# Hybrid mLSTM and stick-breaking layer: the fourth unit's low parts on VectorE in place of GpSimd, and the gates' small product at unit 6 in place of unit 4

## The chip, the cores and the metric

The kernel runs on one core of a Trainium2 chip. The metric is the device time of one execution in microseconds (us), given as the median of the runs. Besides the timed runs there is one profiled execution, from which the trace comes; times inside it count from the start of its span.

A core has TensorE (matmuls; PE in the profile, PEld for the loading of its stationary operand), VectorE (DVE), ScalarE (ACT), GpSimd (POOL) and SyncE (SP), which in this kernel issues nearly all DMAs. Each works through its own instructions in the order of the program, and semaphores make one wait for another.

## What is computed

One layer on x of 512 tokens by 1024 channels, in float32. The reference, cut to its main steps:

```python
h = rmsnorm(x, norm_w)
proj = einsum('bsd,de->bse', h, w_in) + b_in
(mq, mk, mv, mi, mf, mo, mz, sq, sk, sv, sz, gates) = split(proj, split_at)
qk = silu(causal_depthwise_conv(concat([mq, mk]), conv_w, conv_b))
hm = mlstm_chunkwise(q, k, mv, log_i=mi, log_f=log_sigmoid(mf))
y_m = rmsnorm_per_head(hm) * sigmoid(mo) * silu(mz)
os_ = stick_breaking_attention(rmsnorm(sq), rmsnorm(sk), sv)
y_s = os_ * silu(sz)
g_m, g_s = split(sigmoid(gates), 2)
merged = g_m * (y_m @ w_proj_m) + g_s * (y_s @ w_proj_s)
return x + merged @ w_out
```

`mi` and `mf` are four columns each of the input projection; the kernel calls their product the gates (`gates`), which are not the merge gates of the last lines.

## The kernel before

**Three matmuls for one.** Every product of float32 values is made from a high part (the value rounded by a ScalarE copy) and a low part (the value less its high part): high by high, high by low, low by high, added up in PSUM. So each weight tile is loaded by SyncE (`stg`), copied by ScalarE (`wh`) and subtracted by VectorE (`wl`, line 98); normalised x is kept as `hh` and `hl`.

**Units.** The weights are cut into units of 1024 x 128 or 256 x 512 elements, 24 matmuls of 512 columns each. The main loop runs over the units by number (c). In each round it first runs the work that is due at c (`later`, filled by `defer(n, fn)` for n rounds ahead, by `at`, or before the loop), splits the unit two ahead and loads the one four ahead (`ahead`), then issues the unit's matmuls in two halves, with a step of the attention heads between them. Functions due in one round run in the order in which they were put there. This order is the order on every engine.

**The first group.** Units 0 to 3 are the q columns of the attention's first set. They run differently: each token block (tb) takes all of k before the next, so that TensorE can start when the first block of x is normalised. Their weights are split by `first_split` (line 1140): two halves of a unit's tile, each a ScalarE copy (`fh`, line 1146) and a subtraction (`fl`, line 1147) by VectorE or by the engine given as `low`. Units 1 and 3 give GpSimd. Unit i holds k = 2i and 2i + 1, and every token block needs all eight. Around them VectorE and TensorE bring in x: `x_scale` (line 290 is the scaling; its root comes from GpSimd, lines 274 and 275), `x_turn` (line 300 the transposes on TensorE, 302 `hh`, 306 `hl`). The fourth unit's tile lies in the buffer `P5`. Line 347 adds the bias row (`brow`, DMA of line 311) to a finished token block.

**The gates.** `gates_prep` (lines 562 and 563, due at 3) lays the high and low parts of the eight columns into `wg`; `gates` (lines 573 to 581, due at `GATES_START`) multiplies them with `hh` and `hl` in 16 matmuls, copies one half by ScalarE (576), adds on VectorE (578) and stores the results by two SyncE DMAs (580, 581). `gates_scan` reads them from unit 35 on.

**What stands beside them.** The last q block is finished at unit 4. From there `SbSet.turn` runs: at unit 5 it transposes the first half of q on VectorE (`ty`, line 388), at unit 6 `move` sends it to `tz` by 16 SyncE DMAs (line 398), at unit 8 `weight` multiplies it on VectorE (line 402). The second half follows two units later: line 388 at 7, 398 at 8, 402 at 10. The bias row of k is also due at 6, and was put there before the gates. k's blocks are finished at unit 8 and scaled on VectorE (line 369, four steps a block): two blocks at 9, two at 10 behind that `weight`. In unit 10 the first head transposes k on TensorE (line 438).

Of the kernel before, what the change touches and what calls it, by code (L numbers as in the profile page):

```python
# [25 lines left out]

SB_START = [10, 13, 16, 20, 26, 28, 32, 34]
M_START = [52, 56, 70, 76]
GATES_PREP, GATES_START, GATES_SCAN = 3, 4, 35
TURNED = {("q", 0, 0), ("q", 0, 1), ("q", 1, 0), ("q", 1, 1), ("k", 0, 1), ("k", 1, 1)}  # L30
REST = {11, 16, 20, 23, 24, 32, 44, 64}
AHEAD, LOADS = 2, 4
# [3 lines left out]
def tile_hybrid_layer(  # L36
# [16 lines left out]
    nc = tc.nc  # L53
# [21 lines left out]
    def blk(tag, dt=F32, shape=(512,), name=None, p=128):  # L75

        where = mp if tag in MISC else sp
        return where.tile([p] + list(shape), dt, name=name or tag, tag=tag, bufs=BUFS[tag])

    def two(tag, dt=F32, name=None):  # L80

        t = blk(tag, dt, (2, 512), name=name)
        return t[:, 0, :], t[:, 1, :]
# [1057 lines left out]
    def first_split(i, low=None):  # L1141
        u = units[i]
        his = two("qk", FR, name="fh")
        for j in range(2):
            hi, lo = his[j], blk("y", FR, name="fl")
            nc.scalar.activation(hi, u.st[:, j, :], AF.Copy)
            (low or nc.vector).tensor_tensor(lo, u.st[:, j, :], hi.bitcast(F32), op=OP.subtract)  # L1147
            f_w.append((hi, lo))
# [25 lines left out]
    first_split(1, nc.gpsimd)  # L1174
    x_scale(1)
    first_split(2)
    first_split(3, nc.gpsimd)

    f_ps = []

# [121 lines left out]
```

## Time and profile before

| | us |
|---|---|
| median of 3 runs | 691.59 (691.51 to 693.78) |
| the profiled execution | 692.46 |
| its span | 690.7 |
| TensorE busy | 682.2 (99%) |
| VectorE busy | 467.5 (68%) |
| ScalarE busy | 337.1 (49%) |
| GpSimd busy | 115.3 (17%) |

The profiled execution's time is a little longer than its span, which runs from the first to the last instruction. TensorE is busy in nine tenths or more of all but the first and the last of the page's 40 slices. The chain of work that ended last is 94% TensorE's; its other parts lie in the first 38 us and at the end. A timeline row gives the start, the length, the engine, the line and the operation, output and inputs by name and shape; several equal instructions in a row stand as one with their count (x16), and their length is then that from the first start to the last end. In brackets stands how long the engine was idle before it, and who ended that.

### The profile page before, as it was taken

How to read it: one execution, taken by the hardware profiler on the slowest of the kernel's cores; microseconds unless marked ns; L12 is line 12 of the kernel's file. 1: busy time of each engine (PE TensorE's matmuls, PEld its weight loads, DVE VectorE, ACT ScalarE, POOL GpSimd, SP SyncE). 2: the span in 40 equal slices, each digit the busy share in tenths (PEclk: the TensorE clock that was granted, in tenths of full speed). 3: DMA queues.
4: the chain of work that ended last, by engine and by line, in shares of the span. 5: the costliest groups of instructions: out<-in, count | busy, mean ns of one | idle time of the engine just before them, and what ended most of it. 6: DMA issues, size and time to landing. Idle time of an engine off the chain costs nothing.

```text
span 690.7 us, 9388 instructions
## 1 busy us (share of the span) xinstructions
PE 682.2 (99%) x3162; PEld 568.9 (82%) x3162; DVE 467.5 (68%) x817; ACT 337.1 (49%) x631; POOL 115.3 (17%) x268
## 2 busy tenths in 40 slices
PE   7999999999999999999999999999999999999997
PEld 4878888888888888888888888888888888888876
DVE  6745687777997886679834748994352364445997
ACT  6235364576554663244466434447554343344451
POOL 5222022365440310000011110000112000111020
PEclk9999999999999999999999999999999999999999
DMA  7423534535553533553332333434323455489333
GB/s 249 138 92 107 155 108 127 148 71 151 158 149 106 135 106 90 112 121 92 106 108 61 91 105 104 117 92 125 88 62 91 113 179 196 135 194 222 121 82 102
DMA packets 122289, 84.74 MB, mean 123 GB/s; under 512 B 19018, under 2 KB 105956, under 8 KB 122240
## 3 DMA queue, kind: packets, MB, share of 16 engines
q1 hardware_dynamic: 119600, 77.97, 40.2%
q0 software_dynamic: 2496, 6.03, 4.5%
q8 instruction: 25, 0.41, 0.2%
q14 instruction: 24, 0.20, 0.1%
q10 hardware_dynamic: 144, 0.13, 0.1%
HBM read 66.22 MB, written 2.15 MB: 99 GB/s over the span
## 4 chain that ended last, share of the span: by engine, by line
PE 94%; DMA 2%; DVE 2%; POOL 1%; SPq 0%; ACT 0%; issue 0%; DVEq 0%; ACTq 0%
PE dps L92 27%; PE dps L93 27%; PE dps L94 27%; PE aps L93 3%; PE aps L94 3%; PE aps L92 3%; DMA P<-in_w_in_dram 1%; DMA brow<-in_b_in_dram 1%; PE aps L794 1%; PE aps L796 1%; PE aps L795 1%; DVE hl L306 1%; POOL fl L1147 0%; DVE hh L302 0%; DVE wl L98 0%; PE aps L573 0%
## 5 line engine op out<-in xcount | busy, mean ns | idle before, releaser
L98 DVE TENSOR_TENSOR wl<-stg,wh 128x1024 fp32r<-128x1024 f32 x92 | 112.6, 1224 | 107.6 <-ACT wh L97 107.4
L92 PE MATMUL dps<-hh,wh 128*128 128x512 f32 x448 | 175.0, 391 | 0.0
L94 PE MATMUL dps<-hh,wl 128*128 128x512 f32 x448 | 174.4, 389 | 0.0
L93 PE MATMUL dps<-hl,wh 128*128 128x512 f32 x448 | 174.4, 389 | 0.0
L97 ACT ACTIVATE wh<-stg 128x1024 fp32r<-128x1024 f32 x92 | 96.8, 1052 | 65.3 <-PE dps L94 45.1
L94 PEld LDWEIGHTS dps<-hh,wl 128*128 128x128 f32 x448 | 84.1, 188 | 17.7
L93 PEld LDWEIGHTS dps<-hl,wh 128*128 128x128 f32 x448 | 84.2, 188 | 16.8
L92 PEld LDWEIGHTS dps<-hh,wh 128*128 128x128 f32 x448 | 84.1, 188 | 16.8
L92 PE MATMUL dps<-wh,hh 128*128 128x512 f32 x224 | 87.7, 392 | 0.0
L94 PE MATMUL dps<-wh,hl 128*128 128x512 f32 x224 | 87.3, 390 | 0.0
L93 PE MATMUL dps<-wl,hh 128*128 128x512 f32 x224 | 87.2, 389 | 0.0
L94 PEld LDWEIGHTS dps<-wh,hl 128*128 128x128 f32 x224 | 42.0, 188 | 9.0
L92 PEld LDWEIGHTS dps<-wh,hh 128*128 128x128 f32 x224 | 42.1, 188 | 8.3
L93 PEld LDWEIGHTS dps<-wl,hh 128*128 128x128 f32 x224 | 42.1, 188 | 8.2
L687 DVE SCALAR_TENSOR_TENSOR acc<-tmp,vec,acc 128x511 f32<-128x511 f32 (+2 forms) x48 | 36.0, 750 | 1.7
L690 ACT ACTIVATE tmp<-acc 128x512 f32<-128x512 f32 x16 | 10.1, 634 | 50.8 <-DVE acc L687 50.8
L463 POOL TENSOR_SCALAR_AFFINE_SELECT om<-om 128x128 f32<-128x128 f32 x32 | 15.3, 479 | 96.2 <-ACT om L461 96.1
L469 DVE TENSOR_TENSOR_SCAN om<-om 128x512 f32<-128x512 f32 (+3 forms) x32 | 26.7, 834 | 5.5 <-POOL om L463 5.5
L747 POOL TENSOR_SCALAR_AFFINE_SELECT w_all<-om 128x128 f32<-128x128 f32 x16 | 5.7, 386 | 143.6 <-DMA om<-rb_d 129.4
L461 ACT ACTIVATE om<-aps,rq 128x512 f32<-128x512 f32 (+3 forms) x32 | 16.8, 524 | 21.0 <-PE aps L94 21.0
L92 PE MATMUL dps<-yh,wh 128*128 128x512 f32 x64 | 24.9, 389 | 0.0
L93 PE MATMUL dps<-yl,wh 128*128 128x512 f32 x64 | 24.9, 389 | 0.0
(249 smaller groups left out, 1222.2 us busy)
## 6 DMA issues: line engine op xcount, KB each, us to landing
stg<-in_w_in_dram SPq DMA_DIRECT2D x87, 512.0 KB, 3.9
az<-ay SPq DMA_DIRECT2D x128, 40.0 KB, 3.2
stg<-in_w_proj_s_dram SPq DMA_DIRECT2D x8, 512.0 KB, 4.3
B<-in_w_out_dram SPq DMA_DIRECT2D x8, 512.0 KB, 5.8
stg<-in_w_proj_m_dram SPq DMA_DIRECT2D x8, 512.0 KB, 5.5
wl<-stg POOLq DMA_DIRECT2D x8, 512.0 KB, 5.8
tz<-ty SPq DMA_DIRECT2D x72, 32.0 KB, 1.9
brow<-in_b_in_dram SPq DMA_DIRECT2D x8, 256.0 KB, 4.4
```

The costliest lines, as they stand in the source:

```text
L92: nc.tensor.matmul(ps, ah, bh, start=first, stop=False)
L93: nc.tensor.matmul(ps, ah, bl, start=False, stop=False)
L94: nc.tensor.matmul(ps, al, bh, start=False, stop=last)
L97: nc.scalar.activation(hi, src, AF.Copy)
L98: nc.vector.tensor_tensor(lo, src, hi.bitcast(F32), op=OP.subtract)
L306: nc.vector.scalar_tensor_tensor(hl[:, k, ts], tp[:, j * 128:(j + 1) * 128], nw_t[:, k:k + 1], hh[:, k, ts].bitcast(F32), op0=OP.mult, op1 ...
L461: nc.scalar.activation(om[:, 0:n], zp, AF.Sigmoid, scale=rn[:, h:h + 1])
L463: nc.gpsimd.affine_select(out=om[:, ts], in_=om[:, ts], compare_op=OP.is_gt, fill=1.0, base=0, channel_multiplier=1, pattern=[[-1, 128]])
L469: nc.vector.tensor_tensor_scan(back, back, back, 1.0, op0=OP.mult, op1=OP.bypass)
L687: nc.vector.scalar_tensor_tensor(acc[:, j:], t[:, 0:T - j], cw(3 - j, ch), acc[:, j:], op0=OP.mult, op1=OP.add)
L690: nc.scalar.activation(t, acc, AF.Sigmoid)
L794: nc.tensor.matmul(nm[:, 0:258], ph, vh, start=j == 0, stop=False)
```

## The change

Two edits. The fourth unit's low parts are made by VectorE, as the first and the third unit's are, and no longer by GpSimd. The gates' product, with all that `gates` issues, is due at unit 6 and no longer at unit 4; there it comes behind the bias row of k and ahead of `move`. Nothing else differs; what is computed is the same.

```diff
-GATES_PREP, GATES_START, GATES_SCAN = 3, 4, 35
+GATES_PREP, GATES_START, GATES_SCAN = 3, 6, 35
...
     first_split(1, nc.gpsimd)
     x_scale(1)
     first_split(2)
-    first_split(3, nc.gpsimd)
+    first_split(3)
```

## Rows read from the trace of the kernel before

**Rows 1.** Waits of TensorE, whole span: us in total, times, longest

```profile
PE aps L300 <- DVE x L290: 1.4, 2, 1.2
...
PE dps L1190 <- DVE fl L1147: 0.7, 1, 0.7
PE aps L573 <- DVE wg L563: 0.4, 1, 0.4
```

**Rows 2.** Timeline of TensorE, second half of the first unit: start, us

```profile
14.61 0.40 PE L1189 MATMUL dps<-fh,hl 128*128 128x512 f32 x1
...
16.83 0.50 PE L1190 MATMUL dps<-fl,hh 128*128 128x512 f32 x1 [0.73 <-DVE fl L1147]
...
18.55 0.39 PE L1188 MATMUL dps<-fh,hh 128*128 128x512 f32 x1
```

**Rows 3.** Timeline of VectorE and GpSimd, 6 to 18 us

```profile
6.83 1.29 DVE L1147 TENSOR_TENSOR fl<-stg,fh 128x512 fp32r<-128x512 f32 x2
...
12.90 3.32 POOL L1147 TENSOR_TENSOR fl<-P,fh 128x512 fp32r<-128x512 f32 x2 [0.30 <-ACT fh L1146]
13.31 3.46 DVE L1147 TENSOR_TENSOR fl<-stg,fh 128x512 fp32r<-128x512 f32 x2
16.31 0.51 POOL L274 TENSOR_SCALAR xs<-xs 128x1 f32<-128x1 f32 x1
16.70 0.68 DVE L302 TENSOR_TENSOR hh<-aps,nw_t 128x512 fp32r<-128x512 f32 x1
...
17.54 0.19 POOL L274 TENSOR_SCALAR xs<-xs 128x1 f32<-128x1 f32 x1
```

**Rows 4.** Timeline of TensorE around the gates' product

```profile
36.97 0.39 PE L1190 MATMUL dps<-fl,hh 128*128 128x512 f32 x1
37.77 0.47 PE L573 MATMUL aps<-hh,wg 128*128 128x512 f32 x1 [0.41 <-DVE wg L563]
...
41.50 0.39 PE L92 MATMUL dps<-wh,hh 128*128 128x512 f32 x1
```

**Rows 5.** Timeline of SyncE's DMA queue from the gates' stores on

```profile
43.10 0.28 SPq L580 DMA_DIRECT2D i_d<-g  x1
...
45.86 11.03 SPq L398 DMA_DIRECT2D tz<-ty  x16
56.99 1.04 SPq L117 DMA_DIRECT2D stg<-in_w_in_dram  x2
...
68.83 1.15 SPq L117 DMA_DIRECT2D stg<-in_w_in_dram  x2
```

**Rows 6.** Timeline of VectorE: weighting of q's second half, scaling of k

```profile
71.13 0.75 DVE L402 TENSOR_SCALAR tz<-tz,qkw 128x1024 f32<-128x1024 f32 x1
71.80 1.65 DVE L369 TENSOR_SCALAR kraw<-kraw,rk 128x128 f32<-128x128 f32 x8
```

**Rows 7.** Timeline of TensorE in unit 10

```profile
74.14 0.39 PE L92 MATMUL dps<-wh,hh 128*128 128x512 f32 x1
...
76.86 0.60 PE L438 MATMUL aps<-ident,kraw 128*128 128x128 f32 x4
77.22 0.48 PE L92 MATMUL dps<-wh,hh 128*128 128x512 f32 x1
```

**Rows 8.** Timeline of VectorE and TensorE, 20 to 23 us

```profile
20.21 1.41 DVE L290 TENSOR_SCALAR x<-x,xs 128x1024 f32<-128x1024 f32 x2
...
21.05 0.49 PEld L300 LDWEIGHTS aps<-ident,x 128*128 128x128 f32 x3
...
22.55 0.69 DVE L347 TENSOR_TENSOR qraw<-dps,brow 128x512 f32<-128x512 f32 x1 [0.94 <-DMA brow<-in_b_in_dram]
```

**Rows 9.** Timeline of VectorE: the low part of unit 5

```profile
34.80 1.23 DVE L98 TENSOR_TENSOR wl<-stg,wh 128x1024 fp32r<-128x1024 f32 x1 [2.79 <-ACT wh L97]
```

**Rows 10.** Moves (us to landing; ns), then the loads of 56.99 (us to landing)

```profile
DMA to landing us min/median/max: 1.9/1.9/1.9
L398 SPq DMA_DIRECT2D tz<-ty x48: 585/595/1287, 45.9 to 89.9; - x48
DMA to landing us min/median/max: 4.8/4.8/4.8
```

**Rows 11.** Timeline of TensorE at the start of the span

```profile
1.50 4.21 PE L1166 MATMUL dps<-idle 128*128 128x512 f32 x9 [1.50 <-DVE idle L1161]
```

## Prediction before the run

> **What bounds the kernel now.** I read the waits of TensorE first, since the page has it busy for 682.2 of 690.7 us: a change can pay only where TensorE stands still, and can cost only by making it stand still. The view has five entries in the whole span, all before 38 us, three of them shown; the change speaks to the last two [rows 1]. Next I read the timeline of those two places. In the second half of the first unit the matmuls that need the low parts `fl` come late: 14.61 and 18.55 are the starts of the 2nd and the 13th matmul from there [rows 2]. The reason stands beside it: VectorE's two subtractions take 3.46 us while GpSimd does two of its own in 3.32, and 1.29 when nothing runs beside them [rows 3]. The second place is the gates' product, whose first matmul waited 0.41 us for `wg` [rows 4]. Last I read SyncE's queue behind the gates' two stores, because the change puts those stores ahead of other DMAs [rows 5], and then who uses what these DMAs bring [rows 6, 7].
>
> **Low parts by VectorE: what it gives.** The two subtractions of the fourth unit (k 6 and 7) leave GpSimd and join VectorE's two (k 4 and 5). Four at 1.29 / 2 = 0.65 us are 2.6 us, so 13.31 + 2.6 = 15.9 in place of 16.70, where the next `hh` starts: VectorE is 0.8 us earlier although it does twice as much [rows 3]. For TensorE eleven matmul pitches lie between 14.61 and 18.55. Twelve matmuls from 74.14 to 76.86 give a pitch of 0.227 [rows 7], eleven are 2.50, and 3.94 were taken: 1.44 us to gain. The low parts are then ready at 14.0, 14.6, 15.3 and 15.9, the last needed at 16.9, so none is late. What is late next is the transpose of the third token block. TensorE came to it at 21.05 and would now come at 19.6; its input, the scaled `x`, is made from 20.21 on, now 0.8 earlier, and the first of the two takes half of 1.41: done at about 20.1 [rows 8]. So TensorE gains 21.05 - 20.15 = **0.9 us**, and I keep -0.1 to 1.44 as ends (the upper: `x` in time). VectorE itself keeps nothing: its addition at 22.55 waits for the bias row's DMA [rows 8], which SyncE issues as before, so everything from there on VectorE stands where it stood, and is still early enough for a TensorE that is 0.9 us ahead.
>
> [...] The row: one of GpSimd's one-column steps, 0.19 us at 17.54, took 0.51 at 16.31, where VectorE's subtractions had just ended [rows 3]. [...] The row has GpSimd as the one that is held. For the lower end I let two such steps of 0.51 each stop VectorE: 0.9 - 1.0 = -0.1.
>
> **The gates' product two units later: what it gives.** `gates` issues 16 matmuls, one ScalarE copy, one VectorE addition and two SyncE stores. At unit 4 its first matmul started at 37.77 where TensorE could have gone on at 36.97 + 0.23 = 37.20, and the block lasted 3.73 against 16 x 0.227 = 3.63 [rows 4]: 0.57 + 0.10 = **0.67 us** to gain. At unit 6 `wg` has long been there, and units 4 and 5 lie ready (unit 5's low part was made by 36.0 [rows 9], TensorE takes them at 36.3 and 41.7). Unit 4 starts at 37.20 - 0.9 = 36.3, the gates at 36.3 + 2 x 5.44 (24 matmuls each) = 47.2, unit 6 at 50.8 against 41.50 + 10.88 = 52.4. TensorE is 0.9 + 0.67 = **1.57 us ahead**. On ScalarE and VectorE the parts of unit 8 stand behind the gates' two steps, ready at about 54 and wanted at 61.7: hidden. This is the end of what the change gains.
>
> **What it moves on SyncE's queue: the price.** At unit 6 SyncE's order becomes the k bias row, the gates' two stores, and only then the 16 DMAs that move the turned q (first half), the loads of units 10 and 11, 16 more DMAs (second half), the loads of units 12 and 13. The first store, at 43.10, came 1.60 us after the gates' block ended; the two, at 0.28 each and the gaps behind them, hold the queue for some 0.7 [rows 4, 5]. After the change: 50.8 + 1.6 + 0.7 = 53.1 for the first move, where it was 45.86 [rows 5]. From 45.86 to 68.83 the queue issued one instruction after the other (16 moves in 11.03, two loads in 1.04, 16 moves), some 0.67 a move: a queue that is issue-bound doesn't catch up. Its last move was issued at 68.83 - 0.67 = 68.16, which is 22.3 after the first; now 53.1 + 22.3 = 75.4. It lands 1.9 later [rows 10], at 77.3. A move by itself takes 0.595 [rows 10]; if the gap behind it were half as long, 0.64 a move, it is 76.2; I take 77.1.
>
> On VectorE the weighting of that half (`weight`, line 402) stands ahead of the scaling of k's last two token blocks (line 369) in unit 10, and waits for all 16. It was at 71.13, with 1.1 us to spare after the landing at 70.0 [rows 6]; now it is at 77.1. The scaling starts 0.67 later and lasts 1.65; the transposes of k for the first head need the fifth of its eight steps, or the eighth if the wait is for all. TensorE's matmuls go on 1.85 to 2.45 after 77.1, say at 79.1. They went on at 77.22 [rows 7] and could at 77.22 - 1.57 = 75.65. **TensorE stands 3.5 us**, and the sum is 79.1 - 77.22 = **+1.9 us**. The ends: quick pace and fifth step, 78.05, +0.8; 77.3 and eighth step, 79.75, +2.5; with the other ends of the first gain +0.3 and +3.5.
>
> Cover that is used up on the way: the load of unit 10 goes out at 63.9 instead of 56.99, lands 4.8 later [rows 10], and its high and low parts (1.23 for the low [rows 9], the high taken as long) are done by 71.2; TensorE wants them at 74.14 - 1.57 = 72.6. Hidden by 1.4 us; were it gone, that stall would come before the one above and shorten it, not add to it. Unit 12's load, out at 76.1, is ready by the same count at 83.4, wanted at 77.22 + 36 x 0.227 + 1.9 = 87.3. Behind that the waits of the kernel before show no entry for TensorE to the end [rows 1], and I count nothing more.
>
> **Sum.** The profiled execution took 692.46 us (span 690.7), 0.87 above the median of 691.59. 692.46 - 1.57 + 3.5 = 694.4 in that execution's terms, **693.5** as a median. 0.5% is 3.46 us, about what a measurement of this kernel can tell from no change; 1.9 us is 0.27%.
>
> **Rivals.** *The queue doesn't hold TensorE*: the moves land by 73.5, issued quicker in a queue that holds no other transfer. Then only the gains are left, 692.46 - 1.57 = 690.9, 690.0 as a median. Against it: 32 moves beside 4.8-us loads and alone kept the same pace, and VectorE took these steps in the order of the program [rows 5, 6]. 14%.
>
> *The stall costs TensorE its clock*, the one that ends on the slower side. It decides from the point where TensorE stands still long enough in unit 10. The clock column of the page is 1.00 throughout, and the longest wait of TensorE in the part shown is 1.2 us [rows 1], so no row shows a stand of 3.5. [...] One such stretch here would lose half of it, 4.2 / 2 = 2.1 us: 1.9 + 2.1 = +4.0, 696.5, or 695.6 as a median. [...] 15%.
>
> *The first part gives nothing*: the four subtractions don't run at 0.65 (GpSimd's small steps, or the high parts, hold them) and TensorE is no earlier for it. Everything behind shifts with it: 1.9 + 0.9 = +2.8, 694.4 as a median. 9%.
>
> **How the numbers follow.** My forecast, a stall of 2.5 to 4.5 us in unit 10 that eats both gains, has 62%. The range reaches from the first rival's 690.0, less 0.2, to the second's 695.6 and 0.4 more: 689.8 to 696.0. Faster by over 0.5% (below 688.1) has no mechanism: 3% for what I overlooked. Slower by over 0.5% (above 695.05): most of the second rival, and a little from the upper ends of the others, 18%. The rest, 79%, lies within.
>
> **What would show it.** Right, step by step: VectorE's four low parts at 0.65 us from 13.3 on and no wait for `fl` among TensorE's; no wait for `wg`; the gates' stores at about 52.4 and the first move behind them at 53; `weight` at 77 with VectorE idle ahead of it for DMA; a new entry in TensorE's waits at about 75.5, 3 to 4 us for `kraw` of line 369; the clock column 1.00 there. Wrong: no such entry (the queue was quicker), a second entry for `wl` in units 10 to 13 (the loads came late as well), or matmuls at 0.43 behind the stall.

## The result, and the profile after

The changed kernel takes 1.0043 times as long as before (95% interval 1.0031 to 1.0054), about 3.0 us more; the medians are 695.3 and 691.61 us. One of the eight executions took 3680 us: it counts in the median of 695.3 and not in the ratio, and the other seven have a median of 694.93. The forecast was 693.5, +1.9 us: slower by less than 0.5%, and so it is, but by 1.1 us more than the sum said. The profiled execution took 695.68 us, its span is 694.0.

The waits of TensorE after, whole span (us in total, times, longest), to be held against rows 1:

```profile
PE aps L438 <- DVE kraw L369: 2.5, 2, 2.2
PE dps L1188 <- ACT fh L1146: 2.0, 1, 2.0
PE dps L1166 <- DVE idle L1161: 1.5, 1, 1.5
```

The waits for `fl` and for `wg` are gone. A new one has come first in the list: the transposes of k in unit 10 wait for its scaling. The second entry isn't the change's: in this execution the first weights landed later (the first high part at 7.31 us, 6.13 in the profile of before), ahead of anything that was edited. It isn't harmless, though. TensorE stood for it until 10.01, and with that the granted clock fell to 0.50, from about 10.0 to 13.4 by windows of half a us. First TensorE's row, then the windows (stretch, its length, busy time and count of PE, PEld, DVE, ACT and POOL, granted clock, DMA share, GB/s):

```profile
10.01 0.77 PE L1188 MATMUL dps<-fh,hh 128*128 128x512 f32 x1 [1.96 <-ACT fh L1146]
...
10.00:12.00 2.00, 1.99 (x5) 1.68 (x6) 1.96 (x7) 1.90 (x4) 1.95 (x2) 0.50 1.06 424
12.00:14.00 2.00, 2.00 (x8) 1.59 (x7) 1.88 (x6) 1.66 (x4) 0.75 (x2) 0.66 0.98 297
```

The gates' product began 1.2 us later in this execution than in a second one of the same kernel (47.53 and 46.35 us), whose clock did not fall there.

VectorE after, where rows 3 have GpSimd beside it:

```profile
13.57 1.29 DVE L1147 TENSOR_TENSOR fl<-stg,fh 128x512 fp32r<-128x512 f32 x2
14.78 1.29 DVE L1147 TENSOR_TENSOR fl<-P,fh 128x512 fp32r<-128x512 f32 x2
15.98 0.68 DVE L302 TENSOR_TENSOR hh<-aps,nw_t 128x512 fp32r<-128x512 f32 x1
```

Four subtractions in 2.5 us, where two took 3.46. Then SyncE's queue after, for rows 5:

```profile
52.76 0.28 SPq L580 DMA_DIRECT2D i_d<-g  x1
53.09 0.28 SPq L581 DMA_DIRECT2D f_d<-g  x1
53.41 10.35 SPq L398 DMA_DIRECT2D tz<-ty  x16
63.86 1.05 SPq L117 DMA_DIRECT2D stg<-in_w_in_dram  x2
65.01 10.65 SPq L398 DMA_DIRECT2D tz<-ty  x16
75.77 1.15 SPq L117 DMA_DIRECT2D stg<-in_w_in_dram  x2
```

The first move has gone from 45.86 to 53.41 and the order behind it is unchanged, so the last move is out at 75.7, where it was out at 68.7. VectorE, for rows 6, waits for the last of them, and the scaling of k waits with it:

```profile
77.22 0.75 DVE L402 TENSOR_SCALAR tz<-tz,qkw 128x1024 f32<-128x1024 f32 x1 [2.76 <-DMA tz<-ty]
77.89 1.65 DVE L369 TENSOR_SCALAR kraw<-kraw,rk 128x128 f32<-128x128 f32 x8
```

And TensorE in unit 10, for rows 7, where TensorE now stands waiting (the stand, for short):

```profile
75.64 0.38 PE L438 MATMUL aps<-ident,kraw 128*128 128x128 f32 x2
78.23 0.47 PE L438 MATMUL aps<-ident,kraw 128*128 128x128 f32 x1 [2.21 <-DVE kraw L369]
79.02 0.48 PE L438 MATMUL aps<-ident,kraw 128*128 128x128 f32 x1 [0.31 <-DVE kraw L369]
79.14 0.78 PE L92 MATMUL dps<-wh,hh 128*128 128x512 f32 x1
79.72 0.63 PE L93 MATMUL dps<-wl,hh 128*128 128x512 f32 x1
80.14 0.63 PE L94 MATMUL dps<-wh,hl 128*128 128x512 f32 x1
...
88.58 0.39 PE L92 MATMUL dps<-hh,wh 128*128 128x512 f32 x1
```

The transposes of the first two blocks run at once, the third waits for the first step of the scaling, the fourth for the fifth. The unit goes on at 79.14. But then the matmuls start 0.43 apart, not 0.227. The windows of this kernel show what goes with it (columns as above):

```profile
74.00:76.00 2.00, 2.00 (x10) 1.42 (x9) 0.46 (x1) 0.00 (x0) 0.00 (x0) 1.00 0.19 50
76.00:78.00 2.00, 0.02 (x1) 0.00 (x0) 0.78 (x2) 0.00 (x0) 0.00 (x0) 1.00 0.48 89
78.00:80.00 2.00, 1.46 (x4) 1.07 (x5) 1.54 (x8) 0.17 (x1) 0.00 (x0) 0.56 1.13 342
80.00:82.00 2.00, 2.00 (x7) 1.53 (x7) 1.09 (x1) 1.98 (x3) 0.00 (x0) 0.59 1.07 313
82.00:84.00 2.00, 2.00 (x10) 1.68 (x9) 2.00 (x6) 0.69 (x2) 0.00 (x0) 1.00 0.89 239
```

The granted clock fell again after the stand, to 0.50 from about 78.2 to 81.6 by windows of half a us. The 36 matmuls from the end of the stand to the next group's first (79.14 to 88.58) take 9.44 us. In the kernel before the same piece runs from 77.22 [rows 7] to 85.51, 8.29:

```profile
85.51 0.39 PE L92 MATMUL dps<-hh,wh 128*128 128x512 f32 x1
```

The lower clock cost 1.15 us here.

### The profile page after: what moved, and what is told of

It reads as the page before. It is cut to its first block, busy times and chain, and to the rows that moved or that the text cites. A ratio compares the mean times of both kernels' runs of the same rounds, so it can differ in the third digit from the quotient of the medians.

```text
span 694.0 us, 9385 instructions
## 1 busy us (share of the span) xinstructions
PE 684.4 (99%) x3162; PEld 571.3 (82%) x3162; DVE 466.3 (67%) x819; ACT 336.8 (49%) x631; POOL 111.8 (16%) x266
## 4 chain that ended last, share of the span: by engine, by line
PE 94%; SPq 3%; DMA 1%; issue 0%; DVE 0%; ACT 0%; DVEq 0%
PE dps L92 26%; PE dps L93 26%; PE dps L94 26%; PE aps L93 3%; PE aps L94 3%; PE aps L92 3%; SPq L398 3%; PE dps L1188 1%; PE dps L1189 1%; PE dps L1190 1%; DMA stg<-in_w_in_dram 1%; PE aps L794 1%; PE aps L796 1%; PE aps L795 1%; PE aps L300 0%
## 5 line engine op out<-in xcount | busy, mean ns | idle before, releaser
L94 PE MATMUL dps<-yh,wl 128*128 128x512 f32 x64 | 25.0, 391 | 0.0
```

Of the source, the lines that this page charges most:

```text
L94: nc.tensor.matmul(ps, al, bh, start=False, stop=last)
```

## Experiments

Two theories stood against each other at first. The queue: moving the gates' stores ahead of `move` holds 32 DMAs on SyncE, and the last of them holds TensorE. Its rivals: the work that the edits put on VectorE, or the edits simply adding up. Then a second question: whether the clock fell because of the stand. Ratios are to the kernel before, run on the same chip.

### One edit at a time

Only the low parts on VectorE:

```diff
-    first_split(3, nc.gpsimd)
+    first_split(3)
```

> Only the fourth unit's low parts go to VectorE; the gates' product stays at unit 4. Theory: TensorE comes about 0.9 us earlier to the end of the first group, but the gates' first matmul waits there for wg, whose time is set on VectorE by the bias row's DMA and stays at 37.7; so the gain goes into that wait (0.41 grows to about 1.2 us) and the time is that of the kernel before, within 0.3 us. Rival, that the two edits add up: 0.9 us faster, wait for wg unchanged. In either case the four low parts take 0.65 us each.

Measured: 1.0001 (0.9993 to 1.0010), 691.86 us. The four low parts take 0.65 us each and the wait for `fl` is gone, yet no time is gained. Two lines of TensorE's waits in this kernel:

```profile
PE aps L300 <- DVE x L290: 2.0, 2, 1.2
...
PE aps L573 <- DVE wg L563: 0.5, 1, 0.5
```

The wait for `wg` is there still, though not at the 1.2 us expected: in this execution the bias row landed 0.8 us earlier than in the profile of before (21.73 against 22.55 for the addition behind it), and `wg` with it. The direction holds: the edits do not simply add up. Only the gates' product at unit 6:

```diff
-GATES_PREP, GATES_START, GATES_SCAN = 3, 4, 35
+GATES_PREP, GATES_START, GATES_SCAN = 3, 6, 35
```

> Only the gates' product goes to unit 6; GpSimd keeps its low parts. Theory of the queue: TensorE gains 0.6 us at the place of the gates, the stores reach SyncE at about 53.3, the last of the 32 moves lands at about 78, and TensorE stands some 3.5 us in unit 10 for the scaling of k; 2.8 us slower than before, and 4 to 4.5 if the clock falls after the stand. Rival, that the stand in unit 10 comes from the first group's other split: no wait for kraw, 0.6 us faster.

Measured: 1.0055 (1.0043 to 1.0067), 3.8 us slower. SyncE's queue in this kernel:

```profile
52.98 0.28 SPq L580 DMA_DIRECT2D i_d<-g  x1
53.31 0.29 SPq L581 DMA_DIRECT2D f_d<-g  x1
53.63 10.32 SPq L398 DMA_DIRECT2D tz<-ty  x16
```

The moves start as late as in the changed kernel. Its transposes of k, on TensorE's timeline:

```profile
75.86 0.38 PE L438 MATMUL aps<-ident,kraw 128*128 128x128 f32 x2
78.36 0.33 PE L438 MATMUL aps<-ident,kraw 128*128 128x128 f32 x1 [2.12 <-DVE kraw L369]
79.15 0.33 PE L438 MATMUL aps<-ident,kraw 128*128 128x128 f32 x1 [0.46 <-DVE kraw L369]
79.23 0.48 PE L92 MATMUL dps<-wh,hh 128*128 128x512 f32 x1
```

The stand in unit 10 belongs to the gates' place alone; the low parts have no share in it. The granted clock fell behind this stand too, from 80.4 to 83.8.

### Taking the stores, or the moves, off SyncE's queue

The changed kernel with the two stores issued by ScalarE:

```diff
-        nc.sync.dma_start(i_d, g2[0:4, :])
+        nc.scalar.dma_start(i_d, g2[0:4, :])
...
-        nc.sync.dma_start(f_d, g2[32:36, :])
+        nc.scalar.dma_start(f_d, g2[32:36, :])
```

> The changed kernel, with the gates' two stores issued by ScalarE and no longer by SyncE. Theory of the queue: SyncE issues the first move right behind k's bias row at 43 to 46, weight is over by 72, no wait for kraw; both gains are kept: 1.2 to 1.6 us faster than before, clock 1.00 in unit 10. Rival, that it is not the stores that hold the moves but the moves' own work or VectorE's order: the wait for kraw stays at 2 us or more and the time is that of the changed kernel.

Measured: 0.9979 (0.9969 to 0.9989), 1.45 us faster than before and 4.4 faster than the changed kernel, for two stores in another queue. SyncE's queue in this kernel, whose moves start at 43 now:

```profile
43.09 11.50 SPq L398 DMA_DIRECT2D tz<-ty  x16
54.68 1.04 SPq L117 DMA_DIRECT2D stg<-in_w_in_dram  x2
56.72 10.20 SPq L398 DMA_DIRECT2D tz<-ty  x16
```

VectorE's `weight`, with no wait in brackets:

```profile
68.74 0.75 DVE L402 TENSOR_SCALAR tz<-tz,qkw 128x1024 f32<-128x1024 f32 x1
```

Once more, beside two other kernels:

> The changed kernel with the gates' two stores issued by ScalarE, once more, beside the kernel with GpSimd's low parts and the changed kernel on one chip. Theory: 1.4 us faster than before, and 0.7 to 0.9 faster than with GpSimd's low parts. Rival: as fast as that one.

Measured: 0.9984 (0.9976 to 0.9993). This version beats both the kernel before and the changed one. The other way round, the changed kernel with half of the first set's moves issued by GpSimd:

```diff
-                        q = nc.gpsimd if self.s and a % 2 else nc.sync
+                        q = nc.gpsimd if a % 2 else nc.sync
```

> The changed kernel, with half of the moves of q and k of the first set issued by GpSimd, as it does for the second set; SyncE keeps 8 of 16. Theory, that the issuing on SyncE sets when q's second half lands: SyncE's last move is issued at about 65 and lands at 67, weight is over by 70, no wait for kraw, 1.2 to 1.6 us faster than before. Rival, that the transfers themselves are slow: weight stays at 77 and the time at that of the changed kernel.

Measured: 0.9987 (0.9978 to 0.9996), 0.9 us faster, no wait for `kraw`. `weight` started at 72.68, later than the 70 expected: GpSimd issued its half only from 64.14 to 68.5, behind a root that it computes for k. If `weight` waited for the last of these moves, that one landed some 4 us after it was issued (an estimate from 68.5 and 72.68), where SyncE's took 1.9 [rows 10]. It was early enough all the same. Why the gain stayed under the 1.2 us expected was not followed.

### Moving the place, and making the queue longer

The changed kernel with the gates due at 5 (`GATES_START` = 5):

> The changed kernel with the gates' product at unit 5, one unit later than before in place of two. Theory of the queue: the stores go out at about 47.2, the first move at 48 (45.86 before), the last lands at about 72, weight at 72, the scaled k at 74, TensorE wants it at 75.6: no wait, 1.2 to 1.6 us faster than before. Rival, that any later place of the gates costs what it shifts on SyncE: a stand of about 2 us and 0.5 us slower than before.

Measured: 0.9988 (0.9978 to 0.9997), 0.8 us faster, and no wait for `kraw`. The stores go out at 46.01, the moves at 47.68 and 59.94, `weight` starts at 72.09 right behind the landing: this place is the last that fits. Some of its executions show a lower mean clock and 2 us more (692.0 to 692.7 at a mean clock of 0.996 to 0.998, 689.9 to 691.2 at 1.00), which is why it gained less than 1.2 (the others alone gain 1.5); where the clock fell in them was not traced. With the gates due at 8:

> The changed kernel with the gates' product at unit 8. Theory of the queue: the stores now stand ahead of the second half's moves only; they go out at about 63.4, the last move is issued at 74 and lands at 76, weight at 76, the scaled k is there at 77.9 where TensorE wants it at 75.6: a stand of some 2.3 us, shorter than at unit 6 although the place is later; 0.5 to 0.9 us slower than before if the clock holds, 1.5 to 2.5 if it falls. Rival, that a later place simply costs more: a stand over 3.5 us and more than 3 us slower.

Measured: 1.0027 (1.0017 to 1.0036), 1.9 us slower. Stores at 62.86, one half of the moves behind them, a stand shorter than at unit 6, on TensorE's timeline:

```profile
74.87 0.38 PE L438 MATMUL aps<-ident,kraw 128*128 128x128 f32 x2
76.77 0.33 PE L438 MATMUL aps<-ident,kraw 128*128 128x128 f32 x1 [1.52 <-DVE kraw L369]
77.56 0.33 PE L438 MATMUL aps<-ident,kraw 128*128 128x128 f32 x1 [0.45 <-DVE kraw L369]
```

What counted here is what stands behind the stores in SyncE's queue, not how late they come: the first wait for `kraw` is 1.52 with the stores at 62.86 and 16 moves behind them, 2.21 with the stores at 52.76 and all 32. And the clock fell here too, from 78.4 to 81.8. The changed kernel with six more stores behind the two:

```diff
         nc.sync.dma_start(f_d, g2[32:36, :])
+        for i in range(6):
+            nc.sync.dma_start(dp.tile([NH, T], F32, name=f"more{i}"), g2[0:4, :])
```

> The changed kernel with six more stores of the gates' rows behind the two, into tensors nobody reads: 6 x 0.33 = 2.0 us more on SyncE ahead of the moves, and next to no data. Theory, that every microsecond on SyncE there is one of TensorE's stand: weight at 79.2, the wait for kraw 2 us longer than in the changed kernel, matmuls at 0.43 behind it, 2.0 to 2.9 us over the changed kernel. Rival, that the queue has slack behind the stores: no longer than the changed kernel by more than 0.5 us.

Measured: 1.0080 (1.0065 to 1.0094), 5.5 us slower than before, 1.9 to 2.6 more than the changed kernel. The stores took the 1.98 us, and TensorE's longest wait grew by 1.7. `weight` came at 77.88 and not at the 79.2 expected: this execution was at its stores at 51.68, 1.1 us before the first trace of the changed kernel. Against the second one below (stores at 51.58, `weight` at 75.97) it is 1.9 later. The line of SyncE's queue:

```profile
52.34 1.98 SPq L583 DMA_DIRECT2D more<-g  x6
```

The wait is the changed kernel's 2.5 and 2.2, made longer:

```profile
PE aps L438 <- DVE kraw L369: 4.4, 2, 3.9
```

### The clock behind the stand

The changed kernel with the stand filled by work that nobody reads:

```diff
                 else:
+                    if self.s == 0 and h == 0:
+                        fill = att_ps()
+                        for _ in range(15):
+                            nc.tensor.matmul(fill, hh[:, 0, 0:128], hh[:, 0, :], start=True, stop=True)
                     tp = att_ps()
```

> The changed kernel, with 15 matmuls into a spare bank, whose result nobody reads, ahead of the transposes of k in unit 10: 15 x 0.227 = 3.4 us of work in the place of the stand. Theory, that the stand itself lowers the clock: the clock stays 1.00 in unit 10, the wait for kraw is under 0.6 us, the next unit goes on at about 79.1 as in the changed kernel, and the time is 1.9 to 2.2 us over the kernel before, 1 to 1.4 us less than the changed kernel. Rival, that the slow matmuls behind the stand come from what runs at that time on the other engines and DMAs: they stay at 0.43, and the time is that of the changed kernel, 3 us over before.

Measured: 1.0025 (1.0016 to 1.0034), 1.7 us slower than before. TensorE waits for no `kraw`, and after the fill the matmuls soon start 0.227 apart. Its windows (stretch, length, busy time and count of PE, granted clock, DMA share, GB/s) at the place where the changed kernel has 0.56 and 0.59:

```profile
78.00:80.00 2.00, 2.00 (x13) 1.00 1.13 341
80.00:82.00 2.00, 2.00 (x10) 1.00 0.99 293
```

The DMAs are about as busy there as in the changed kernel; TensorE's stand is gone, and with it the lower clock. Over all executions that is worth 1.2 us (2.97 less 1.73) of the 3.0; against the second timing of the changed kernel, below, it is 1.9. The fill itself runs a little longer than the stand: it lets TensorE go on at 78.26, where the second trace below goes on at 77.84. And the changed kernel itself once more:

> The changed kernel itself, once more. Theory of the stand and the clock: 2.5 to 3.5 us slower than before, 4 to 5 slower than with ScalarE's stores; a wait for kraw of 2 to 3 us and a granted clock near 0.5 in part of 78 to 82 us. Rival, that the falling clock was an accident of one execution: clock 1.00 there and 1.7 to 2.0 us slower than before, as with the stand filled.

Measured: 1.0052 (1.0040 to 1.0064), 3.6 us slower. But the profiled execution, one of the faster with 694.1 us, kept its clock. TensorE's timeline there, and one window (columns as for the fill):

```profile
74.46 0.38 PE L438 MATMUL aps<-ident,kraw 128*128 128x128 f32 x2
76.97 0.33 PE L438 MATMUL aps<-ident,kraw 128*128 128x128 f32 x1 [2.13 <-DVE kraw L369]
77.75 0.33 PE L438 MATMUL aps<-ident,kraw 128*128 128x128 f32 x1 [0.46 <-DVE kraw L369]
77.84 0.47 PE L92 MATMUL dps<-wh,hh 128*128 128x512 f32 x1
...
86.13 0.39 PE L92 MATMUL dps<-hh,wh 128*128 128x512 f32 x1
...
78.00:80.00 2.00, 2.00 (x10) 1.00 1.08 333
```

The same wait, and behind it 8.29 us for the piece that took 9.44. So neither statement of the expectation holds alone: the clock falls behind this stand in some executions and not in others, and the median lies with those of a lower mean clock (693.8 and 694.1 at 0.999 and 1.00; 695.4 to 696.4 at 0.997 and 0.998).

A mean doesn't say where the clock fell, and the first trace shows that it can fall at the start as well. So the count over all executions is the better test. A mean clock of 0.998 or less stands in 20 of the 32 executions of the four kernels with the stand (the changed one in both its timings, the gates alone, the gates at 8, six more stores), in 9 of 74 of the six without it, and in 3 of 76 of the kernel before that ran beside them. By this count it is the stand that made the lower clock likely here. What it costs one execution is less sure: 1.15 us in the piece worked out above, but the changed kernel's executions of the lower mean took 2.0 us more than its others (695.8 and 693.8). Falls at the start may be the rest; that was not shown.

### The gates' place without the queue, and the low parts with it

The kernel with ScalarE's stores, but GpSimd's low parts:

```diff
-    first_split(3)
+    first_split(3, nc.gpsimd)
```

> The gates' product at unit 6 with its stores issued by ScalarE, and the fourth unit's low parts still on GpSimd: the gain of the gates' place by itself, with SyncE's queue out of the way. Theory, that the gates' place gains 0.6 us and the low parts 0.9 once the wait for wg is gone: 0.5 to 0.7 us faster than before, the waits for fl still there, none for wg and kraw, and 0.7 to 0.9 slower than the same kernel with the low parts on VectorE. Rival, that the low parts on VectorE gain nothing anywhere (alone they gave nothing): as fast as that kernel, 1.4 us faster than before.

Measured: 1.0000 (0.9992 to 1.0009), against 0.9984 for the same kernel with the low parts on VectorE. Half of the expectation fell: the gates' place alone does not show its 0.6 us, to within 0.6. The other half held: the low parts are worth 1.1 us once the gates are out of the way (1.1 by the ratios, 1.6 by the medians).

## Why the prediction was right, and where its sizes were off

**Low parts.** The step held in its mechanism. VectorE's four took 0.65 each, and `hh` started at 15.98 for 15.9. GpSimd's small steps took 0.42 and 0.88 us beside them (0.19 and 0.55 to 0.56 beside other work of VectorE or none), and VectorE's kept 0.65: it was GpSimd that was held. That its steps stop VectorE, the 1.0 us of my lower end, was an estimate that no run shows: VectorE's four kept 0.65 in all six traces read there, and it took nothing from the sum. The row had said so already, though I misread it: at 16.31 VectorE's subtractions had not just ended, they ran until 16.77 [rows 3], and GpSimd's step ended with them, at 16.82. The 0.9 is 1.1 in the comparison of the last two kernels. Left out was that it pays only with the other edit: alone it gave nothing.

**Gates' product.** This term was mis-sized. I took 0.67 us from one execution, 0.87 above the median, whose bias row had landed late (its addition at 22.55 is the latest of the nine traces read there, 21.01 the earliest) and kept `wg` late; over many executions the gates' place alone gives 0.0, with 0.6 either way. Together the two edits gain 1.1 to 1.45 us, where I had 1.57. Neither gives anything alone. That fits two arrivals of about the same time, TensorE at the gates' place and `wg`: moving one alone changes nothing. This reading agrees with the four measurements; the arrival of `wg` in untraced executions was not seen.

**SyncE's queue.** Right in each step of the mechanism: stores at 52.8 (forecast 52.4), first move at 53.4 (53.1), `weight` at 77.2 (77.1), TensorE going on at 79.14 (79.1), after the fifth of eight steps. The time lost there, 3.5 us, was 3.1 in the trace (79.14 less 75.64 and the transposes' own 0.36): after its late start this execution came to the place 0.35 us later than forecast. In the second execution it was 3.0. That the times on the clock agree to 0.4 us is partly luck: this execution had been held up at its start, and in the second one the same steps came at 51.6, 52.2, 76.0 and 77.84. What moved the queue moved the time: 2 us more on it cost 1.9 to 2.6 us, taking the stores off gave 4.4 and 4.7 back.

**The covers** held. There is no wait for `wl` in units 10 to 13; unit 10's low part was there at 70.1 (forecast 71.2). Three other traces (the gates alone, GpSimd's moves, the changed kernel's second) have one wait of 0.2 to 0.6 us for a DMA of `wl` after 640 us, far behind the change; it was not followed.

**The clock** is what the sum lacked. Without its fall the forecast of +1.9 was met: 1.7 with the stand filled, and 2.1 in the five executions of the changed kernel with a mean clock of 0.999 or 1.00. Here too some luck helped: the gain was put too high by 0.1 to 0.5 us and the stand by 0.4 to 0.5, and the two nearly cancel. I had kept the falling clock as a rival at 15%, and by the mean clocks it came in most executions of the changed kernel (0.998 or less in 8 of 13), at 1.15 us in the one worked out, not 2.1. The 2.1, with which the range ended at 696.0, was half of the 4.21 us of nine matmuls at the start of the span [rows 11]. I took that stretch for one at half the clock, from its pace alone (0.47 us each against 0.227); no run shows it, and the granted clock stands at 1.00 there:

```profile
2.00:4.00 2.00, 2.00 (x6) 1.52 (x6) 0.00 (x0) 0.59 (x2) 0.00 (x0) 1.00 0.92 283
```

In its place the traces whose clock fell showed 0.50 for some 3.4 us behind the stand, with matmuls 0.43 apart. The chance was too low because I reasoned from a wait of 1.2 us, the longest shown, that left the clock alone [rows 1] (it ended at 13.45, and the granted clock is 1.00 from 12 to 18); between that and 3.5 I had no row. The trace after has one: a wait of 1.96 us at its start, and the clock down behind it. Of the five traces with the stand in unit 10 four have the clock down behind it, after 2.8 to 5.2 us; in the fifth, after 3.38, it stayed at 1.00.

## What to carry to other kernels

When work is moved to a later point, its DMAs go with it: look at what each queue holds behind them there, because here two stores of 0.28 us each, which waited for their result, held the 32 moves and the loads among them. The queue, which issued for 22 us with next to no pause, passed the delay on to its last move almost whole (7.55 us at the first move, 6.9 at the last); another engine's queue, or a place one unit earlier, avoided it here. Two stalls at the same place may have hidden each other here: of two edits that each gave nothing alone (1.0001 and 1.0000), the pair gave over 1 us (0.9979 and 0.9984, with ScalarE's stores).

## What the runs showed that I had not expected

TensorE's stand in unit 10 cost more than its length in most executions (by the mean clocks, 20 of 32), and not the same in each. From the first transpose of k to the matmuls that go on, TensorE did four short transposes in 2.8 us (gates at unit 8), 3.5 (the changed kernel) and 5.2 (six more stores), and in each trace the granted clock fell to 0.50 for some 3.4 us, at a price of 1.15 us in the one worked out above. With the gates alone the stretch was 3.37 us and the clock fell; in the second trace of the changed kernel it was 3.38, and the clock stayed at 1.00. What decides between the two is open. A second surprise is how the subtractions on VectorE and GpSimd slowed each other here. VectorE's took 0.65 us alone, and GpSimd's 1.28 beside VectorE's `hh` and `hl`, as this line of the kernel before shows; side by side they took about 1.7 both [rows 3].

```profile
9.14 2.55 POOL L1147 TENSOR_TENSOR fl<-stg,fh 128x512 fp32r<-128x512 f32 x2 [3.01 <-ACT fh L1146]
```

Four on VectorE alone took 2.5 us, less than two of them beside GpSimd's two.
